# Where the scan's decay matrices come from: running sums spread by memory in place of segment sums by TensorE

## The chip, the cores and the metric

The kernel runs on one core of a Trainium2 chip. The metric is the device time of one execution, in microseconds (us). The kernel before took 1235.95 us (median of 3 runs, 1234.91 to 1236.33). Its engines are TensorE (PE, with its weight loads as PEld), VectorE (DVE), ScalarE (ACT), GpSimd (POOL) and SyncE (SP, which issues every DMA of this kernel).

## The reference

One layer of a hybrid encoder over 1024 prompt tokens and 64 sample tokens, width 1024. A projection gives z, x/B/C, dt and the input of a pooling branch; x/B/C go through a causal convolution and SiLU; then the chunked scan, a gate and an output projection; a SwiGLU feed-forward; and a gated per-layer embedding. The change is in the scan, whose core is:

```python
acum = cumsum(dtc * a, axis=time)             # running sum of the decay exponents of a chunk, per head
diff = acum[..., :, None] - acum[..., None, :]
lmat = exp(where(causal, diff, -inf))         # decay from token j to token i of the chunk
y_diag = einsum('bcign,bcjgn,bcgrij,bcjgrp->bcigrp', cc, bc, lmat, xdt)
decay_end = exp(acum[..., -1:] - acum)        # and chunk_decay = exp(acum[..., -1])
```

There are 8 heads. All of `dtc * a` is negative, so `acum` falls along a chunk.

## The kernel before

The kernel holds activations as [feature, token]. The 1088 tokens stand in four column groups of 272 for the large products. Each fp32 operand of those is split into a high and a low float32r part, and a product is three passes (high x high, high x low, low x high), run by `run` (L472, matmuls on L477). The scan takes 128 tokens at a time: 8 chunks of the prompt (c = 0 to 7) and one of the 64 sample tokens (c = 8).

The order of the instructions on PE, DVE, ACT and POOL is written out in advance by a planner, the class `Layout`. Jobs are Python generators that yield either a condition or a request: an engine, a cost in us, and a time to wait (`("A", 0.24, 0)`: ACT, 0.24 us, at once; "D" is DVE, "P" PE, "S" the issue of a DMA). The planner keeps a clock that moves on with each large product and with each "P" request, takes the ready jobs by priority, and emits an instruction when it gives a job its turn. So the costs decide the order, and the engines then run in this order, each waiting on semaphores for what it needs. DMAs stand on SP's single queue. What a DMA's reader is told to wait for is worked out by `dma` (L381) from a number of columns that the call names.

Scan chunks are jobs between the large products of the input projection. Before them, `dt_chain` (L957) computes for all 72 columns (9 chunks x 8 heads) the step `dt` and the exponent `dta`, and from three products with constant matrices (`le`: token j <= i, `gt`: token j > i, `ones`; L1018) by one exponential each `ea` (decay since the chunk's start), `dend` (to its end) and `cdec` (of the whole chunk).

`decay(c)` (L1036) prepares the decay matrices of a chunk on ACT: for each of 8 heads it multiplies the 128x128 matrix `le` by the head's column of `dta`, once for the high part (`dh`) and once for the low part (`dl`): 16 instructions. `ssd(c)` (L1049) then does, in this order: transposes and B/C products on PE (L1063 to L1068), `xdt`, `bk`, `cbm` (L1071 to L1079), **the segment sums on PE (L1089)**, four matmuls of 512 columns of the constant `gt_r` with `dh` and `dl`, into two PSUM banks; `xw` (L1092); the exponential of those banks into `e` on ACT (L1098); the skip term on ACT (L1103); the products with the state and for the new state (L1109, L1115); `e` times `cbm` (L1119), `yo`, the state's decay on DVE; and the chunk's output on PE (L1140, L1144). After its end the job of the next chunk is spawned; `decay(c + 1)` is spawned after `xw` of chunk c.

The chunks' results are gated by z (`z_job`, L1279; `gate`, L1296), and the output projection, the feed-forward (L1624, with a fast matrix scheme of seven products) and the embedding follow. Beside the scan runs the pooling branch (`pool_post`, L1190; its products on L1230).

Of the kernel before, what the change touches and what calls it, by code (L numbers as in the profile page):

```python
# [7 lines left out]
F32 = mybir.dt.float32  # L8
F32R = mybir.dt.float32r
I32 = mybir.dt.int32  # L10
AF = mybir.ActivationFunctionType
ALU = mybir.AluOpType
PSUM = bass.MemoryType.PSUM

P = 128
# [6 lines left out]
NC = len(CH)  # L22
# [300 lines left out]

@with_exitstack
def trunk(ctx, tc, xT, par, wmix, wdt, poolw, wout, wff, wdn, wpg, wpp, pT, ssm0,
          yT, ssm_o, conv_o, pool_o, h1_d, pool_d, e_d, af_d):
    nc = tc.nc
    ve, ac, gp, pe, sy = nc.vector, nc.scalar, nc.gpsimd, nc.tensor, nc.sync
    ET = mybir.EngineType
# [2 lines left out]
    const = ctx.enter_context(tc.tile_pool(name="const", bufs=1))  # L332
# [14 lines left out]
    banks = Banks()  # L347
    nts = Sem(NNT)
# [7 lines left out]
    def jbank(name):  # L356

        b = banks.take()
        return banks.hold(psall[:, b, :], b)
# [14 lines left out]
    def nt(name, dtype=F32):  # L374
        nts.take()
        return ntp.tile([P, CW], dtype, tag="nt", name=name)
# [4 lines left out]
    def dma(dst, src, cols):  # L381
        sy.dma_start(dst, src)
        return lay.load(cols)
# [4 lines left out]
    def pcol(name, i=None, n=1):  # L388
        a, b = _PCOLS[name]
        if i is None:  # L390
            return cp[:, a:b]
        return cp[:, a + i:a + i + n]

    gt_r = const.tile([P, P], F32R, name="gt_r")
    ident = pcol("ident")
    ones = pcol("ones")
    le = pcol("le")
    gt = pcol("gt")
# [439 lines left out]
            wsem.give()  # L838

    def gt_job():  # L840
        yield ("A", 0.2, 10)
        ac.copy(gt_r, pcol("gt"))
        yield ("D", 0.16)
        ve.tensor_tensor(pcol("pool_b"), pcol("pool_b"), pcol("pool_scale"), ALU.mult)

    spawn(w0_job(), 0)
# [88 lines left out]
    NH = 8 * NSSD  # L935

    def ct_(name):
        return keep.tile([P, NH], F32, name=name)

    dt, dta, dta_l, ea, dend, cdec = (ct_(n) for n in ("dt", "dta", "dta_l", "ea", "dend", "cdec"))  # L940
    dta_h = keep.tile([P, NH], F32R, name="dta_h")
    pwr = nt("pwr0"), nt("pwr1")
    dt_done = []

# [12 lines left out]
    def dt_chain():  # L957
        yield lambda: sdt[0] == 1 + NC
        yield banks.ok
        psd = jbank("psd")  # L960
        yield ("P", 1.0, 2)
        for c in range(NSSD):
            L = P if c < 8 else DEC
            pe.matmul(psd[:L, 8 * c:8 * c + 8], dtT[:, P * c:P * c + L], pcol("dtsum"),
                      start=True, stop=True)
        yield room_nt(3)
        s1, s2, s3 = (nt(f"sp{i}")[:, :NH] for i in range(3))
        d = ("D", 0.2, 0)
        yield ("D", 0.14, 1)
        ve.memset(dt, 0.0)  # L970
        by_c = "p (c h) -> p c h"
        ve.tensor_tensor(dt[:, :64].rearrange(by_c, h=8), psd[:, :64].rearrange(by_c, h=8),
                         pcol("dt_bias").unsqueeze(1).broadcast_to([P, 8, 8]), ALU.add)
        yield d
        ve.tensor_tensor(dt[:DEC, 64:72], psd[:DEC, 64:72], pcol("dt_bias")[:DEC], ALU.add)
        banks.give(psd)

        yield d
        ve.scalar_tensor_tensor(s1, dt, -1.0, dt, ALU.mult, ALU.max)
        yield ("A", 0.46)  # L980
        ac.activation(s1, s1, AF.Exp, scale=-1.0)
        ac.activation(ea[:, :8], pcol("a_log"), AF.Exp)
        yield ("D", 0.14, 2)
        ve.tensor_scalar(s2, s1, 2.0, None, ALU.add)
        yield ("D", 0.5)
        ve.reciprocal(s2, s2)
        yield d
        ve.tensor_tensor(s1, s1, s2, ALU.mult)
        yield d
        ve.tensor_tensor(s2, s1, s1, ALU.mult)  # L990
        yield d
        ve.tensor_scalar(s3, s2, 1.0 / 17, 1.0 / 15, ALU.mult, ALU.add)
        for k in (13, 11, 9, 7, 5, 3, 1):
            yield d
            ve.tensor_tensor(s3, s3, s2, ALU.mult)
            yield d
            ve.tensor_scalar(s3, s3, 1.0 / k, None, ALU.add)
        yield d
        ve.tensor_tensor(s3, s3, s1, ALU.mult)
        yield d  # L1000
        ve.tensor_scalar(dt, dt, 0.0, None, ALU.max)
        yield d
        ve.scalar_tensor_tensor(dt, s3, 2.0, dt, ALU.mult, ALU.add)
        ve.memset(dt[DEC:, 64:72], 0.0)
        yield d
        ve.scalar_tensor_tensor(dta.rearrange(by_c, h=8), dt.rearrange(by_c, h=8), -1.0,
                                ea[:, :8].unsqueeze(1).broadcast_to([P, NSSD, 8]), ALU.mult, ALU.mult)
        yield ("A", 0.2)
        ac.copy(dta_h, dta)
        yield ("D", 0.14)  # L1010
        ve.tensor_tensor(dta_l, dta, dta_h.bitcast(F32), ALU.subtract)
        for _ in range(3):
            nts.give()
        yield banks.ok
        psc = jbank("psc")
        yield ("P", 0.4, 2)
        for n, m in enumerate((le, gt, ones)):
            pe.matmul(psc[:, 128 * n:128 * n + NH], m, dta, start=True, stop=True)  # L1018
        yield ("A", 0.7)
        for n, o in enumerate((ea, dend, cdec)):  # L1020
            ac.activation(o, psc[:, 128 * n:128 * n + NH], AF.Exp)
        banks.give(psc)
        dt_done.append(1)

    spawn(dt_chain(), P_DTC)
# [8 lines left out]
    DD = {}  # L1034

    def decay(c):  # L1036

        L = DEC if c == 8 else P
        for g in range(2):
            hg = slice(8 * c + 4 * g, 8 * c + 4 * g + 4)  # L1040
            for nm, src in (("dh", dta_h.bitcast(F32)), ("dl", dta_l)):
                for h in range(4):
                    yield ("A", 0.24, 0)
                    if not h:
                        d = sp.tile([P, 4, P], F32R, tag=nm, bufs=2, name=f"{nm}{c}_{g}")
                    ac.activation(d[:L, h, :L], le[:L, :L], AF.Identity, scale=src[:L, hg][:, h:h + 1])
                DD[c, g, nm] = d

    def ssd(c):  # L1049
        sample, first = c == 8, c == 0  # L1050
# [28 lines left out]
        ve.tensor_tensor(cbm[:L, :, :L], pb[:L, 256:256 + 2 * L].rearrange("p (g i) -> p g i", g=2),  # L1079
                         le[:L, :L].unsqueeze(1).broadcast_to([L, 2, L]), ALU.mult)  # L1080
        banks.give(pb)
        yield lambda: banks.free >= 2 and (c, 1, "dl") in DD
        pgs = [jbank(f"pg{c}_{g}") for g in range(2)]
        es = []
        pvs = [p_[:L, :4 * L].rearrange("p (h i) -> p h i", h=4) for p_ in pgs]
        yield ("P", 0.9, 0)
        for g in range(2):
            for j, nm in enumerate(("dh", "dl")):
                pe.matmul(pvs[g], gt_r[:L, :L], DD[c, g, nm][:L, :, :L], start=j == 0, stop=j == 1)  # L1089
        yield ("D", 0.7, 0)  # L1090
        xw = sp.tile([P, 8, 64], F32, tag="xw", bufs=1, name="xw" + n)
        ve.tensor_tensor(xw[:L], xdt[:L], dend[:L, h8].unsqueeze(2).broadcast_to([L, 8, 64]), ALU.mult)  # L1092
        if c + 1 < NSSD:
            spawn(decay(c + 1), P_DEC)
        for g in range(2):
            yield ("A", 0.55, 1 - g)
            e = sp.tile([P, 4, P], F32, tag="e", name=f"e{c}_{g}")
            ac.activation(e[:L, :, :L], pvs[g], AF.Exp)  # L1098
            banks.give(pgs[g])
            es.append(e)  # L1100
        for b in range(4):
            yield ("A", 0.24, 0)
            ac.activation(xs[:, b, t0:t0 + L], xs[:, b, t0:t0 + L], AF.Identity, scale=pcol("d_skip", b))  # L1103
# [1244 lines left out]
```

## Time and profile before

| | |
|---|---|
| median of 3 runs | 1235.95 us |
| the profiled execution | 1235.68 us, its span 1233.8 us |
| PE busy, weight loads busy | 1208.4 us (98%), 1186.7 us (96%) |
| DVE, ACT, POOL busy | 873.2 us (71%), 596.1 us (48%), 69.4 us (6%) |
| segment sums (L1089) | 36 matmuls between 133 and 266 us |

The span runs from the first to the last instruction; the execution's time is 1.9 us more. An engine's share says how long it was busy, not whether others waited for it. PE is the one that is almost never idle; where a stage shows it busy all the time, only what PE itself does, or what it is made to wait for, can move the end. The views used below are the page's busy times, the busy times by stage, single instructions in order of time, the groups of instructions by line, the waits, and the DMA issues with their time to landing. For PE a matmul's length in the views includes a modelled end that overlaps the next matmul, so what a matmul costs in a stream is read from start to start.

### The profile page before, as it was taken

What the parts mean: (1) busy time and instruction counts of PE and PEld (TensorE: products, weight loads), DVE (VectorE), ACT (ScalarE), POOL (GpSimd) and SP (SyncE); (2) the same over time, 40 slices, a digit from 0 to 9 for tenths busy, and PEclk for the clock granted to TensorE, in tenths of its full rate; (3) what the DMA queues carried; (4) which work ended last, traced back from release to release, by engine and by line L of the source; (5) the groups of instructions that cost most, each with busy time, mean ns of one, the idle gap of its engine ahead of it and who ended that gap; (6) DMA issues with size and microseconds to landing.
All of it is one profiled execution on the core that took longest, in us unless ns stands there. A gap on an engine that the chain in (4) does not pass through costs nothing.

```text
span 1233.8 us, 23914 instructions
## 1 busy us (share of the span) xinstructions
PE 1208.4 (98%) x9676; PEld 1186.7 (96%) x9676; DVE 873.2 (71%) x1572; ACT 596.1 (48%) x1196; POOL 69.4 (6%) x56
## 2 busy tenths in 40 slices
PE   8999999999999999999999999999999999999997
PEld 6999999999999899999999999999999999999996
DVE  6696866785788786775767677666656555688875
ACT  6365667975546544444444444344433111356543
POOL 2000000111222100000000000000000000001111
PEclk8999999999999999999999999999999999999998
DMA  6121112124444233533443444336987666334422
GB/s 225 41 73 35 46 53 74 37 83 135 157 146 161 94 110 138 168 128 133 174 145 116 151 150 169 118 120 226 397 325 254 247 233 233 124 111 128 135 84 82
DMA packets 72399, 177.82 MB, mean 144 GB/s; under 512 B 8545, under 2 KB 16993, under 8 KB 72289
## 3 DMA queue, kind: packets, MB, share of 16 engines
q1 hardware_dynamic: 72288, 176.30, 41.5%
q8 instruction: 75, 1.23, 0.4%
q14 instruction: 36, 0.29, 0.1%
HBM read 117.31 MB, written 58.96 MB: 143 GB/s over the span
## 4 chain that ended last, share of the span: by engine, by line
PE 63%; DVE 3%; DMA 1%; ACT 0%; POOL 0%; issue 0%; DVEq 0%; ACTq 0%; POOLq 0%; SPq 0%
PE psall L1624 54%; PE psall L477 6%; PE psall L494 2%; POOL mixf L1414 0%; DVE f L1887 0%; PE psall L512 0%; DMA raw_pg<-in_wpg_dram 0%; DVE mixf L1439 0%; DVE sq_f L609 0%; PE psall L550 0%; DMA e_dram<-e 0%; DVE mixf L1408 0%; DVE mixf L1471 0%; DVE h_T L401 0%; PE psall L2107 0%
## 5 line engine op out<-in xcount | busy, mean ns | idle before, releaser
L477 PE MATMUL psall<-x,w_in 128*128 128x272 f32 x1440 | 194.9, 291 | 0.0
L477 PEld LDWEIGHTS psall<-x,w_in 128*128 128x128 f32 x1440 | 184.7, 188 | 4.0 <-issue 2.4
L1887 DVE TENSOR_TENSOR f<-f,psall 128x544 f32<-128x544 f32 (+1 forms) x96 | 60.7, 637 | 69.2 <-PE psall L1624 67.5
L1624 PE MATMUL psall<-h_T,w_g_S 128*128 128x272 f32 x792 | 103.0, 290 | 2.2 <-DVE h_T L401 1.8
L1624 PEld LDWEIGHTS psall<-h_T,w_g_S 128*128 128x128 f32 x792 | 101.3, 191 | 2.6 <-DVE h_T L401 2.0
L1624 PE MATMUL psall<-al_T,w_d_S 128*128 128x272 f32 x768 | 100.1, 288 | 0.9 <-DVE f L1887 0.5
L1624 PE MATMUL psall<-h_T,w_u_S 128*128 128x272 f32 x792 | 100.7, 287 | 0.0
L1624 PEld LDWEIGHTS psall<-h_T,w_u_S 128*128 128x128 f32 x792 | 99.6, 188 | 0.0
L1624 PEld LDWEIGHTS psall<-al_T,w_d_S 128*128 128x128 f32 x768 | 97.7, 188 | 1.6 <-DVE f L1887 0.7
L477 PE MATMUL psall<-mix,w_out 128*128 128x272 f32 x720 | 93.3, 289 | 0.0
L477 PEld LDWEIGHTS psall<-mix,w_out 128*128 128x128 f32 x720 | 90.9, 188 | 0.0
L1624 PE MATMUL psall<-al_B,w_d_A 128*128 128x272 f32 x528 | 72.1, 289 | 2.6 <-DVE w_d_A L401 2.6
L477 PE MATMUL psall<-h,w_pg 128*128 128x272 f32 x576 | 74.3, 289 | 0.0
L477 PEld LDWEIGHTS psall<-h,w_pg 128*128 128x128 f32 x576 | 72.7, 188 | 0.0
L1624 PEld LDWEIGHTS psall<-al_B,w_d_A 128*128 128x128 f32 x528 | 68.4, 188 | 3.1 <-DVE w_d_A L401 3.1
L1624 PE MATMUL psall<-h_B,w_g_A 128*128 128x272 f32 x528 | 70.2, 288 | 0.1
L1624 PE MATMUL psall<-h_B,w_u_A 128*128 128x272 f32 x528 | 69.7, 288 | 0.0
L1624 PEld LDWEIGHTS psall<-h_B,w_g_A 128*128 128x128 f32 x528 | 67.7, 188 | 0.4 <-ACT e L1807 0.4
L1624 PEld LDWEIGHTS psall<-h_B,w_u_A 128*128 128x128 f32 x528 | 67.5, 188 | 0.0
L1552 ACT CAST w_d_A<-raw_d 128x512 fp32r<-128x512 f32 (+3 forms) x44 | 22.3, 522 | 69.9 <-PE psall L1624 35.1
L1552 ACT CAST w_d_S<-raw_d 128x512 fp32r<-128x512 f32 (+3 forms) x54 | 26.5, 532 | 57.7 <-DVE raw_d L1576 33.6
L2073 POOL TENSOR_TENSOR f<-f,sq_f 128x544 f32<-128x544 f32 x5 | 7.4, 1482 | 726.8 <-DVE f L2070 721.4
(405 smaller groups left out, 2290.1 us busy)
## 6 DMA issues: line engine op xcount, KB each, us to landing
af_dram<-a_T SPq DMA_DIRECT2D x88, 272.0 KB, 2.3
al_T<-af_dram SPq DMA_DIRECT2D x44, 544.0 KB, 5.6
af_dram<-a_B SPq DMA_DIRECT2D x66, 272.0 KB, 2.3
al_B<-af_dram SPq DMA_DIRECT2D x33, 544.0 KB, 5.8
raw_g<-in_wff_dram SPq DMA_DIRECT2D x22, 512.0 KB, 4.2
raw_u<-in_wff_dram SPq DMA_DIRECT2D x22, 512.0 KB, 3.6
raw_in<-in_wmix_dram SPq DMA_DIRECT2D x15, 512.0 KB, 3.6
raw_d<-in_wdn_dram SPq DMA_DIRECT2D x14, 512.0 KB, 4.9
```

The costliest lines, as they stand in the source:

```text
L477: pe.matmul(out, lhsT, rhs, start=i == 0, stop=i == n - 1)
L494: pe.matmul(out, w.v(wi, k), act.v(xi, k, L), start=first and n == 0, stop=not left and n == 2)
L1552: ac.copy(v[:, 0], src)
L1624: pe.matmul(d[:, p - q.ps[0], :], w.v(wi, k), u.b(bf, xi, p, k), start=start and not k and not wi and not xi, stop=k == u.ks - 1 and wi == ...
L1887: ve.tensor_tensor(v[:, sl], v[:, sl], src[:, pl], ALU.add)
L2073: gp.tensor_tensor(v, v, hr, ALU.add)
```

## The change

The segment sum from token j to token i is the difference of two running sums, `acum[i] - acum[j]`. The changed kernel no longer forms it with `gt_r` on PE. `dt_chain` copies the `le` product to `acum` on ACT, transposes it on PE into the free end of the same bank (72 rows of heads, 128 tokens), copies that to SBUF on DVE, and stores it to a DRAM tensor `ac_d`. `decay(c)` loads the 8 rows of its chunk back, each lane getting the same 8 x 128 numbers, into `e` (three buffers); ACT then computes for each head `relu(acum[j] - acum[i])`, with `acum[j]` as the lane's bias (8 instructions of 128 columns), and `exp` of its negative (2 instructions of 512 columns). What `ssd` multiplies by `cbm` is this `e`; `cbm` is masked by `le`, so the entries that the relu cut to zero fall away. `gt_r`, `dta_h`, `dta_l`, the 16 products of ACT per chunk, the four matmuls and their two banks are gone. `dt_done`, which starts the scan, is now set after the store's landing as the planner reckons it.

```diff
-    gt_r = const.tile([P, P], F32R, name="gt_r")
...
-    dt, dta, dta_l, ea, dend, cdec = (ct_(n) for n in ("dt", "dta", "dta_l", "ea", "dend", "cdec"))
-    dta_h = keep.tile([P, NH], F32R, name="dta_h")
+    dt, dta, acum, ea, dend, cdec = (ct_(n) for n in ("dt", "dta", "acum", "ea", "dend", "cdec"))
...
-        s1, s2, s3 = (nt(f"sp{i}")[:, :NH] for i in range(3))
+        s1w, s2, s3 = (nt(f"sp{i}") for i in range(3))
+        s1, s2, s3, s1w = s1w[:, :NH], s2[:, :NH], s3[:, :NH], s1w[:, NH:NH + P]
...
-        yield ("A", 0.2)
-        ac.copy(dta_h, dta)
-        yield ("D", 0.14)
-        ve.tensor_tensor(dta_l, dta, dta_h.bitcast(F32), ALU.subtract)
-        for _ in range(3):
+        for _ in range(2):
             nts.give()
         yield banks.ok
         psc = jbank("psc")
         yield ("P", 0.4, 2)
         for n, m in enumerate((le, gt, ones)):
             pe.matmul(psc[:, 128 * n:128 * n + NH], m, dta, start=True, stop=True)
+        yield ("A", 0.2)
+        ac.copy(acum, psc[:, :NH])
+        yield ("P", 0.2, 0)
+        pe.transpose(psc[:NH, 384:512], acum, ident)
+        yield ("D", 0.2, 0)
+        ve.tensor_copy(s1w[:NH], psc[:NH, 384:512])
+        yield ("S", 0, 0)
+        at = dma(ac_d, s1w[:NH], 1)
         yield ("A", 0.7)
         for n, o in enumerate((ea, dend, cdec)):
             ac.activation(o, psc[:, 128 * n:128 * n + NH], AF.Exp)
         banks.give(psc)
+        yield ("A", 0.02, at)
+        nts.give()
         dt_done.append(1)
...
     def decay(c):
         L = DEC if c == 8 else P
+        yield ("S", 0, 0)
+        e = sp.tile([P, 8, P], F32, tag="e", bufs=3, name=f"e{c}")
+        at = dma(e, ac_d[8 * c:8 * c + 8].partition_broadcast(P), 2 * P)
+        for h in range(8):
+            yield ("A", 0.39, at if not h else 0)
+            ac.activation(e[:L, h, :L], e[:L, h, :L], AF.Relu, bias=acum[:L, 8 * c + h:8 * c + h + 1], scale=-1.0)
         for g in range(2):
-            hg = slice(8 * c + 4 * g, 8 * c + 4 * g + 4)
-            for nm, src in (("dh", dta_h.bitcast(F32)), ("dl", dta_l)):
-                for h in range(4):
-                    yield ("A", 0.24, 0)
-                    if not h:
-                        d = sp.tile([P, 4, P], F32R, tag=nm, bufs=2, name=f"{nm}{c}_{g}")
-                    ac.activation(d[:L, h, :L], le[:L, :L], AF.Identity, scale=src[:L, hg][:, h:h + 1])
-                DD[c, g, nm] = d
+            yield ("A", 0.55, 0)
+            ac.activation(e[:L, 4 * g:4 * g + 4, :L], e[:L, 4 * g:4 * g + 4, :L], AF.Exp, scale=-1.0)
+        DD[c] = e
...
-        yield lambda: banks.free >= 2 and (c, 1, "dl") in DD
-        pgs = [jbank(f"pg{c}_{g}") for g in range(2)]
-        es = []
-        pvs = [p_[:L, :4 * L].rearrange("p (h i) -> p h i", h=4) for p_ in pgs]
-        yield ("P", 0.9, 0)
-        for g in range(2):
-            for j, nm in enumerate(("dh", "dl")):
-                pe.matmul(pvs[g], gt_r[:L, :L], DD[c, g, nm][:L, :, :L], start=j == 0, stop=j == 1)
...
-        for g in range(2):
-            yield ("A", 0.55, 1 - g)
-            e = sp.tile([P, 4, P], F32, tag="e", name=f"e{c}_{g}")
-            ac.activation(e[:L, :, :L], pvs[g], AF.Exp)
-            banks.give(pgs[g])
-            es.append(e)
+        yield lambda: c in DD
+        es = DD[c][:, :4], DD[c][:, 4:]
```

The planner's order changes with it, from the end of `dt_chain` to the first groups of the output projection; after that the instructions of every engine stand as before. Three places show it. In the rows, names stand without buffer numbers, a trailing number is an instruction's own, and `x4` is a run of four.

On PE, in the kernel before, chunk 2 from the B/C products (L1067) to the products with the state (L1109) and for the new state (L1115):

```order
L1067 MATMUL psall<-ct,bt 128x128 x2
L477 MATMUL psall<-x_11_99,w_in_1458 128x272 x4
...
L477 MATMUL psall<-x_11_103,w_in_1458 128x272 x3
L1089 MATMUL psall<-dh_0_1828,gt_r 128x512
L1089 MATMUL psall<-dl_0_1834,gt_r 128x512
L1089 MATMUL psall<-dh_1_1848,gt_r 128x512
L1089 MATMUL psall<-dl_1_1873,gt_r 128x512
L477 MATMUL psall<-x_11_103,w_in_1458 128x272
...
L1109 MATMUL psall<-state_1846,ct 128x256 x2
L1115 MATMUL psall<-xw_1965,bk_1932 128x256 x2
```

On PE, in the changed kernel, chunk 3 over the same stretch (L1073 are the B/C products now, L1103 and L1109 those with and for the state):

```order
L1073 MATMUL psall<-ct,bt 128x128 x2
L476 MATMUL psall<-x_00_99,w_in_1452 128x272 x2
...
L476 MATMUL psall<-x_01_92,w_in_1591 128x272 x4
L476 MATMUL psall<-x_10_93,w_in_1591 128x272
L1103 MATMUL psall<-state_1894,ct 128x256 x2
L1109 MATMUL psall<-xw_1997,bk_1985 128x256 x2
```

The four long matmuls are gone, and fewer matmuls of the input projection stand between the two ends: 57 before, 39 now. Over the whole scan, the projection's work between one chunk's start and the next shrinks, and the ninth chunk's output stands 196 matmuls earlier in PE's order, 35 of them those that are gone less the one that is added.

On ACT, in the changed kernel, from chunk 1's `bk` (L1082) to chunk 2's; `e_1710` is chunk 2's decay, L1049 the relu and L1052 the exponential, L1097 the skip term, L1211 a step of the pooling branch:

```order
L1082 COPY bk_1684<-psall 128x256
L1097 ACTIVATE xs<-xs,cp 128x128 x4
L1049 ACTIVATE e_1710<-e_1710,acum 128x128 x3
L1211 CAST ph_1739<-s_3_1687 128x1103
L1049 ACTIVATE e_1710<-e_1710,acum 128x128 x5
L1052 ACTIVATE e_1710<-e_1710 128x512 x2
L447 CAST w_in_1795<-raw_in_1467 128x1024
L1230 ACTIVATE po_0_1800<-psall,cp 128x272
L1082 COPY bk_1829<-psall 128x256
```

Chunk 2's decay is whole before chunk 2's `bk`; before, its exponential stood behind `bk` and behind the segment sums. The table loads of ACT go from 19 to 15.

On SP, in the changed kernel, the store of the running sums and the broadcast loads (`e_1353`, `e_1576`, `e_1710`, `e_1853`, `e_2010` are chunks 0 to 4):

```order
L382 DMA raw_in_1199<-in_wmix_dram 128x1024
L382 DMA ac_dram<-sp_898 72x128
L382 DMA e_1353<-ac_dram 128x1024
L382 DMA e_1576<-ac_dram 128x1024
L382 DMA raw_in_1341<-in_wmix_dram 128x1024
L382 DMA e_1710<-ac_dram 128x1024
L382 DMA raw_in_1467<-in_wmix_dram 128x1024
L382 DMA out_conv_dram<-conv_out 128x48
L382 DMA raw_in_1605<-in_wmix_dram 128x1024
L382 DMA e_1853<-ac_dram 128x1024
L382 DMA e_2010<-ac_dram 128x1024
```

Ten DMAs are new: a store of 36 KB, on which the first load waits, and nine loads that write 512 KB each. The first three have a buffer at once; a later one waits until the chunk three before it has used its own. Weight loads (`raw_in`) stand between and behind them on the queue.

## Rows read from the trace of the kernel before

**Rows 1.** The page's busy time of each engine: us, share of the span, instructions.

```profile
...
PE 1208.4 (98%) x9676; PEld 1186.7 (96%) x9676; DVE 873.2 (71%) x1572; ACT 596.1 (48%) x1196; POOL 69.4 (6%) x56
```

**Rows 2.** Busy by stage: PE, PEld, DVE, ACT, POOL (instructions), clock, DMA share, GB/s.

```profile
...
150.00:170.00 20.00, 20.00 (x156) 19.14 (x155) 14.64 (x24) 13.68 (x40) 0.00 (x0) 1.00 0.16 55
...
190.00:210.00 20.00, 20.00 (x167) 18.85 (x166) 14.98 (x24) 14.38 (x32) 0.00 (x0) 1.00 0.19 61
210.00:230.00 20.00, 18.65 (x157) 17.73 (x156) 14.68 (x26) 17.33 (x46) 4.30 (x4) 1.00 0.20 60
230.00:250.00 20.00, 19.81 (x168) 18.87 (x167) 15.41 (x38) 18.54 (x50) 3.20 (x4) 1.00 0.13 36
...
290.00:310.00 20.00, 20.00 (x171) 20.00 (x171) 9.09 (x29) 7.60 (x18) 0.00 (x0) 1.00 0.30 94
```

**Rows 3.** PE in order of time, chunk 0: start us, us, instruction, count.

```profile
...
133.46 0.40 PE L1089 MATMUL psall<-dh,gt_r 128*128 128x512 f32 x1
133.69 0.39 PE L1089 MATMUL psall<-dl,gt_r 128*128 128x512 f32 x1
...
134.39 1.80 PE L477 MATMUL psall<-x,w_in 128*128 128x272 f32 x13
```

**Rows 4.** PE in order of time, chunk 8.

```profile
...
265.13 0.33 PE L1089 MATMUL psall<-dh,gt_r 64*64 64x256 f32 x1
...
265.74 1.01 PE L477 MATMUL psall<-x,w_in 128*128 128x272 f32 x6
```

**Rows 5.** Instructions of L1089: ns min/median/max, first and last start us, forms.

```profile
...
L1089 PE MATMUL psall<-dh,gt_r x18: 278/396/478, 133.5 to 265.4; 128*128 128x512 f32 x16, 64*64 64x256 f32 x2
```

**Rows 6.** PE in order of time, the products of the running sums.

```profile
...
106.92 0.79 PE L1018 MATMUL psall<-dta,cp 128*128 128x72 f32 x6
107.51 1.75 PE L477 MATMUL psall<-x,w_in 128*128 128x272 f32 x12
```

**Rows 7.** PE in order of time, four transposes of chunk 0.

```profile
...
130.10 0.60 PE L1063 MATMUL psall<-cp,xs 128*128 128x128 f32 x4
130.54 0.38 PE L1065 MATMUL psall<-cp,bt 128*128 128x128 f32 x2
```

**Rows 8.** ACT by group, 100 to 300 us: busy us, mean ns, idle before.

```profile
...
L1046 ACT ACTIVATE dh<-cp,dta_h 128x128 fp32r<-128x128 f32 x64 | 21.0, 395 | 0.0
...
L1098 ACT ACTIVATE e<-psall 128x512 f32<-128x512 f32 x16 | 8.7, 595 | 5.9 <-PE psall L1089 5.9
L1098 ACT ACT_TABLE_LOAD x6 | 7.7, 1283 | 0.1
```

**Rows 9.** ACT in order of time, chunk 6.

```profile
...
216.58 1.12 ACT L1217 CAST ph<-s 128x1103 fp32r<-128x1103 f32 x1 [2.26 <-DVE s L1212]
217.72 1.28 ACT L1098 ACT_TABLE_LOAD   x1
...
221.27 1.28 ACT L1288 ACT_TABLE_LOAD   x1
```

**Rows 10.** DVE in order of time, chunk 6.

```profile
...
223.03 0.44 DVE L1292 TENSOR_TENSOR xs<-xs,z 128x272 f32<-128x272 f32 x1 [3.64 <-ACT z L1288]
223.38 1.86 DVE L1119 TENSOR_TENSOR e<-e,cbm 128x512 f32<-128x512 f32 x2
```

**Rows 11.** PE in order of time, chunk 6's output.

```profile
...
226.00 0.63 PE L1140 MATMUL psall<-cp,yo 128*128 128x128 f32 x4 [1.35 <-DVE yo L1128]
```

**Rows 12.** DVE's waits, 150 to 170 us: us in total, times, longest.

```profile
...
DVE xs L1156 <- PE psall L1144: 3.3, 1, 3.3
```

**Rows 13.** ACT in order of time, end of the chain of dt.

```profile
...
107.79 1.28 ACT L1021 ACT_TABLE_LOAD   x1 [2.03 <-PE psall L1018]
```

**Rows 14.** DMA issues: count, KB each, median us from issue to landing.

```profile
...
al_B<-af_dram SPq DMA_DIRECT2D x33, 544.0 KB, 5.8
...
raw_in<-in_wmix_dram SPq DMA_DIRECT2D x15, 512.0 KB, 3.6
...
out_conv_dram<-conv_out SPq DMA_DIRECT2D x1, 24.0 KB, 1.5
```

More of the change, by code (lines that the diff above doesn't have):

```diff
@@ L325, in trunk @@
 def trunk(ctx, tc, xT, par, wmix, wdt, poolw, wout, wff, wdn, wpg, wpp, pT, ssm0,
-          yT, ssm_o, conv_o, pool_o, h1_d, pool_d, e_d, af_d):
+          yT, ssm_o, conv_o, pool_o, h1_d, pool_d, e_d, af_d, ac_d):
     nc = tc.nc
@@ L840, in gt_job @@
     def gt_job():
-        yield ("A", 0.2, 10)
-        ac.copy(gt_r, pcol("gt"))
-        yield ("D", 0.16)
+        yield ("D", 0.16, 10)
         ve.tensor_tensor(pcol("pool_b"), pcol("pool_b"), pcol("pool_scale"), ALU.mult)
@@ L2332 @@
     af_d = [nc.dram_tensor(f"af_{j}_dram", (7, P, 4 * CW), F32).ap() for j in range(NFF // 2)]
+    ac_d = nc.dram_tensor("ac_dram", (72, P), F32).ap()
     with tile.TileContext(nc) as tc:
@@ L2335 @@
               ap["wff"], ap["wdn"], ap["wpg"], ap["wpp"], [ap[f"p{c}"] for c in range(NC)], ap["ssm0"],
-              [ap[f"o_y{c}"] for c in range(NC)], ap["o_ssm"], ap["o_conv"], ap["o_pool"], h1_d, pool_d, e_d, af_d)
+              [ap[f"o_y{c}"] for c in range(NC)], ap["o_ssm"], ap["o_conv"], ap["o_pool"], h1_d, pool_d, e_d, af_d, ac_d)
     r = run_bass_kernel_spmd(nc, [feed], core_ids=[0])
```

## The prediction, made before the changed kernel was run

> **What bounds the kernel now.** The page's busy times come first: PE is busy 98% of the span, DVE 71%, ACT 48% [rows 1]. The busy time by stage, second, says where: PE works 20.00 of 20 us at full clock at 150 and 190 us, in the middle of the scan, while DVE has 14.64 and 14.98 and ACT 13.68 and 14.38 [rows 2]. From 210 to 250 us PE loses 1.35 and 0.19 us, where ACT is fullest (17.33 and 18.54); after the scan, at 290 us, PE is at 20.00 again with DVE at 9.09 and ACT at 7.60 [rows 2]. So in this stretch PE's own work sets the time, and others wait for it: between 150 and 170 us DVE stood 3.3 us for one output of the scan [rows 12]. Third, single instructions in order of time give what each removed or added one costs PE, from start to start. Fourth, the groups on ACT and the landing times of DMAs show whether what is added can hide.
>
> **PE, removed.** In chunk 0 the first segment sum starts at 133.46, the second at 133.69, and the projection goes on at 134.39: 0.23 us for one matmul of 512 columns, 0.93 us for four [rows 3]. Sixteen of the eighteen `dh` matmuls have 512 columns, and there are as many `dl` [rows 5]: eight chunks x 0.93 = 7.44 us. Chunk 8's four take 265.13 to 265.74, 0.61 us [rows 4]. Together 8.05 us.
>
> **PE, added.** One transpose of `acum`. Four transposes take 130.10 to 130.54, so 0.11 us each [rows 7]. It waits for ACT's copy. Before, ACT starts on the bank 0.87 us after PE's first of the three products (106.92 to 107.79) [rows 6, 13]; a copy of 72 columns is no row here, and lies between nothing and the 0.60 us of a 512-column exponential [rows 8]; I take 0.25. So `acum` is there 1.1 us after the products start. PE has 0.59 us of products, then six projection matmuls in the new order, each about 0.13 (12 in 1.75 us, less the last one's modelled end) [rows 6]: 1.4 us. The wait is nothing; ACT held by one convolution step would make it about 1.1 us, the length of a cast of similar width [rows 9]. Behind it on PE stands only the projection. Net for PE: 8.05 - 0.11 = 7.94 us.
>
> A rule of the Trainium skill speaks against the size of this term. "TensorE: Matmul & The Clock Gate", section "Back-to-back issue gap", gives about 131 ns per matmul of 512 columns in a stream of weight loads and matmuls, less than the 216 ns of one alone. By it, 32 x 0.131 + 0.61 = 4.8 us would go, and the gain would be 4.7 instead of 7.9, an estimate. The trace does not agree: each of its 512-column matmuls, with a weight load of its own, takes 0.23.
>
> **ACT.** Per chunk, 16 products of 128 columns become 8 relus of 128, and the two exponentials stay. The 64 full-size `dh` products keep ACT busy 21.0 us, 0.33 each [rows 8]. A relu with a per-lane bias does not occur; the nearest row is that product with a per-lane scale, and I take its 0.33 (0 to twice that: from 5 us less to no change in a chunk). So ACT does 8 x 0.33 = 2.6 us less a chunk, and four table loads of 1.28 us go [rows 8]. ACT's time lies beside PE's, and pays only where PE waited for it. Such a place is chunk 6: the pooling cast, then a table load at 217.72, the two exponentials, the skip term and the next table load at 221.27 [rows 9] kept DVE waiting 3.64 us for a z, so that `e` times `cbm` began at 223.38 [rows 10] and PE stood 1.35 us for `yo` [rows 11]. In the changed kernel the exponential is no longer between the segment sum and this product, but table loads still alternate with z's SiLU. I credit half, 0.7 us (0 to 1.54, all that PE loses from 210 to 250 us).
>
> **DMA and SP.** The store of 36 KB and chunk 0's load follow each other: nearest are 1.5 us (24 KB) and 3.6 us (512 KB of weights) [rows 14], so about 5 us. SP stands still for the first of these, with one weight load behind the first two broadcast loads. The running sums exist at about 108 us; chunk 0 wanted its segment sums at 133.46 [rows 3], so some 20 us of projection cover the round trip. Each later load is issued when the chunk three before has been used, with a chunk every 16.5 us (133.5 to 265.4 over eight) [rows 5]; after the change perhaps 13 us. It lands in 3.6 us, or 5.8 as in the busiest stretch [rows 14]: covered either way. That 128 lanes read the same 4 KB has no row; only a landing beyond some 13 us would be seen. Ten DMAs write 4.7 MB where the DMA engines are busy 0.13 to 0.20 [rows 2].
>
> **DVE.** One subtraction of 72 columns goes, one copy of 128 comes: nothing. But the chunks stand closer: per chunk 57 projection matmuls became 39 between the same two steps, 18 x 0.13 = 2.3 us, plus the 0.93. That is 3.3 of 16.5 us. DVE's share of 73 to 75% in the scan rises, to at most 93% if all its work moved together. I take 0.7 us of new waits on PE for this (0 to 4). After the scan, all engines' orders are as before and PE is full at 290 us, so what is gained is kept.
>
> **Sum.** The profiled execution took 1235.68 us: a span of 1233.8 and 1.9 around it. 1235.68 - 7.94 - 0.7 + 0.7 = 1227.7. The median of the runs is 0.27 above the profiled one: 1228.0 us.
>
> **Rivals.**
> 1. *Denser chunks make PE wait for DVE (slower).* Place: before each chunk's output (L1140), PE waits for `yo`, which is behind the two products with `cbm` (0.93 us each [rows 10]). With chunk starts 13 us apart each chunk would do what chunk 6 did, 1.35 us [rows 11]: nine times, 12.2 us, against 7.94: 1235.95 + 4.2 = 1240 us. It decides from 7.94 / 9 = 0.88 us per chunk on. For it: DVE is the second fullest engine. Against: the exponential that made chunk 6 late is out of this chain, and DVE waited for PE elsewhere. Chance 0.11.
> 2. *PE is paid by the matmul, not by the column.* Then 36 x 0.13 = 4.7 us go: 1231.3 us. For it: projection matmuls come every 0.13 us at 272 columns. Against: rows 3. The rule quoted above would give the same. Chance 0.05.
> 3. *The gain is given back.* PE reaches the output projection 8 us earlier and waits there for gates, whose chain of DVE and ACT has its own pace: about 1235.5 us. For it: ACT is nearly full from 230 to 250 us [rows 2]. Against: the scan ends still earlier against the projection than before, and ACT has less to do. Chance 0.08.
> 4. *The change's loads do not hide*, because the shared 4 KB comes slowly or the queue stands. At twice a chunk's 13 us, ACT would lose over 10 us on most of the chunks: above 1250 us. Against: rows 14. Chance 0.03.
>
> **How the numbers follow.** The forecast has 0.73, with its own range from 1225.5 (all of the 1.54 saved, no new waits, and 1 us for runs) to 1232 (4 us of new waits). Faster by over 0.2% (2.5 us, about what a measurement of this kernel can tell from no change) are the forecast and rival 2: 0.78; within it rival 3: 0.08; slower rivals 1 and 4: 0.14. The range to 1234 leaves out rivals 1 and 4 and most of 3.
>
> **What would show it.** Right: no 512-column matmul on PE between 130 and 270 us, PE at 20 of 20 through the scan, the first group of the feed-forward about 8 us earlier; relus of 0.3 to 0.4 us on ACT that wait for no DMA; broadcast loads landing in about 4 us. Wrong: waits of PE for `yo` or `e` beyond 0.9 us a chunk (rival 1); relus that wait for the load (rival 4); PE idle before the output projection (rival 3); a scan that ends 8 us earlier and an end that does not.

## The result, and the profile after

The changed kernel takes 1224.74 us in the median of 5 runs (1223.88 to 1226.61), beside 1235.95 for the kernel before. The ratio is 0.9916, 95% interval 0.9901 to 0.9932: 8.4 to 12.2 us less. Timed again later it gave 1226.25 us, ratio 0.9923 (0.9908 to 0.9937). So it is faster, as forecast; the forecast of 1228.0 was 3.3 us too slow, and the first median lies 0.8 us below the 1225.5 that the forecast gave as its own low end, while the second lies above it. Single runs of one kernel differ by some 2 us along with their mean granted clock: at 0.996 the kernel before took 1233.55 to 1234.08 us and the changed one 1223.88, at 0.993 they took 1235.50 to 1237.74 and 1226.21 to 1226.77.

The page of the changed kernel, busy time of each engine, to be held against [rows 1]:

```profile
...
PE 1200.6 (98%) x9641; PEld 1180.8 (96%) x9641; DVE 872.8 (71%) x1572; ACT 571.8 (47%) x1119; POOL 69.4 (6%) x56
```

PE has 7.8 us less, ACT 24.3 us less, DVE the same. The profiled run took 1226.61 us, the longest of its five, with a span of 1224.8: 9.0 us under the span before. Where these 9 us went shows best if the execution is cut at two marks that both kernels have: the first product of the `dt` chain (`psd`) and the first output projection. PE in the kernel before, the instructions of L964 and then the time order (columns as in [rows 5] and [rows 3]):

```profile
...
L964 PE MATMUL psall<-cp,ct x18: 170/256/256, 69.2 to 71.1; 128*128 128x8 f32 x16, 128*64 128x8 f32 x2
...
276.50 1.67 PE L1952 MATMUL psall<-mix,w_out 128*128 128x272 f32 x12
```

The same two marks in the changed kernel:

```profile
...
L960 PE MATMUL psall<-cp,ct x18: 170/256/256, 70.0 to 71.9; 128*128 128x8 f32 x16, 128*64 128x8 f32 x2
...
267.78 1.42 PE L1946 MATMUL psall<-mix,w_out 128*128 128x272 f32 x10
```

Between the marks: 276.50 - 69.2 = 207.3 us before, 267.78 - 70.0 = 197.8 after, 9.5 less. From the second mark to the end of the span: 957.3 before, 957.0 after. So in these two profiles the whole gain is made in the scan and none is given back. The first mark stands 0.8 us later in the changed run; over the runs below it stands between 68.9 and 71.2 us whatever was edited, so 1 to 2 us of difference ahead of it mean nothing.

The same stretches as in [rows 2], changed kernel:

```profile
...
150.00:170.00 20.00, 20.00 (x171) 19.12 (x170) 15.54 (x27) 11.17 (x31) 0.00 (x0) 1.00 0.33 108
190.00:210.00 20.00, 20.00 (x172) 19.12 (x171) 14.95 (x25) 14.00 (x28) 0.00 (x0) 1.00 0.33 113
210.00:230.00 20.00, 19.78 (x154) 18.80 (x153) 14.19 (x24) 17.75 (x46) 3.29 (x4) 1.00 0.19 57
230.00:250.00 20.00, 20.00 (x188) 18.04 (x187) 18.19 (x44) 12.53 (x34) 4.71 (x4) 1.00 0.29 87
290.00:310.00 20.00, 20.00 (x165) 20.00 (x164) 6.36 (x8) 9.12 (x16) 0.00 (x0) 1.00 0.34 107
```

PE stays at 20.00, and the two gaps from 210 to 250 us (1.35 and 0.19) are down to 0.22. That is all that PE waits between 70 and 270 us, by its waits (us in total, times, longest):

```profile
...
PE psall L1224 <- DVE pl L400: 0.2, 1, 0.2
```

So 7.9 (PE's work, net) + 1.54 (idle time gone) - 0.22 (new) = 9.3 of the 9.5 us. The step that the change removed is gone: PE in order of time, chunk 0 (compare [rows 3]):

```profile
...
132.29 2.79 PE L476 MATMUL psall<-x,w_in 128*128 128x272 f32 x21
134.91 1.02 PE L1109 MATMUL psall<-xw,bk 128*128 128x256 f32 x4
```

Projection runs up to the state product without a 512-column matmul between. And the new step on PE (compare [rows 6]):

```profile
...
107.01 0.78 PE L1011 MATMUL psall<-dta,cp 128*128 128x72 f32 x6
107.60 1.00 PE L476 MATMUL psall<-x,w_in 128*128 128x272 f32 x6
108.43 0.27 PE L1016 MATMUL psall<-cp,acum 128*72 128x128 f32 x1
```

No bracket behind L1016: the transpose waits for nothing, since six projection matmuls lie between. ACT in order of time at this place (compare [rows 13]):

```profile
...
107.83 0.22 ACT L1014 COPY acum<-psall 128x72 f32<-128x72 f32 x1 [3.52 <-PE psall L1011]
...
114.52 2.46 ACT L1049 ACTIVATE e<-e,acum 128x128 f32<-128x128 f32 x8 [2.48 <-DMA e<-ac_dram]
```

The copy took 0.22 us (taken: 0.25). The last row is the only relu that waits for a load, chunk 0's. SP's queue in order of time:

```profile
...
109.05 0.38 SPq L382 DMA_DIRECT2D ac_dram<-sp  x1
110.55 0.82 SPq L382 DMA_DIRECT2D e<-ac_dram  x2
```

From the store's issue to the first relu it is 5.5 us (taken: about 5), and chunk 0's product with `cbm` comes 21 us later, at 135.9. Landing times (compare [rows 14]):

```profile
...
e<-ac_dram SPq DMA_DIRECT2D x9, 512.0 KB, 3.9
```

ACT by group, 100 to 300 us (compare [rows 8]):

```profile
...
L1049 ACT ACTIVATE e<-e,acum 128x128 f32<-128x128 f32 x64 | 20.6, 392 | 2.5 <-DMA e<-ac_dram 2.5
...
L1052 ACT ACTIVATE e<-e 128x512 f32<-128x512 f32 x16 | 9.4, 622 | 0.0
...
L1052 ACT ACT_TABLE_LOAD x4 | 5.1, 1283 | 0.1
```

A full relu keeps ACT busy 20.6 / 64 = 0.32 us, as the product did (0.33). Note the last column of the exponentials: ACT no longer stands 5.9 us for a segment sum. Where chunk 6 was late is seen on three engines (compare [rows 9 to 11]). ACT in order of time, the exponentials of this chunk:

```profile
...
204.94 1.15 ACT L1052 ACTIVATE e<-e 128x512 f32<-128x512 f32 x2
```

DVE in order of time, their product with `cbm`:

```profile
...
212.62 1.28 DVE L1113 TENSOR_TENSOR e<-e,cbm 128x512 f32<-128x512 f32 x2
```

PE in order of time, the chunk's output:

```profile
...
217.57 0.60 PE L1134 MATMUL psall<-cp,yo 128*128 128x128 f32 x4
```

The exponentials end at 206.1, 6.5 us before DVE multiplies them with `cbm`, and 11 us before PE takes `yo`; neither row has a wait. In the kernel before, they and two table loads stood between z and its SiLU, for which DVE waited 3.64 us.

### The profile page after: what moved, and what is told of

Its sections match the earlier page's. It is cut to its first block, busy times and chain, and to the rows that moved or that the text cites. A ratio compares the mean times of both kernels' runs of the same rounds, so it can differ in the third digit from the quotient of the medians.

```text
span 1224.8 us, 23784 instructions
## 1 busy us (share of the span) xinstructions
PE 1200.6 (98%) x9641; PEld 1180.8 (96%) x9641; DVE 872.8 (71%) x1572; ACT 571.8 (47%) x1119; POOL 69.4 (6%) x56
## 4 chain that ended last, share of the span: by engine, by line
PE 62%; DVE 3%; DMA 2%; POOL 0%; ACT 0%; issue 0%; DVEq 0%; ACTq 0%; POOLq 0%; SPq 0%
PE psall L1618 54%; PE psall L476 6%; PE psall L493 2%; DMA al_B<-af_dram 1%; POOL mixf L1408 0%; DMA raw_d<-in_wdn_dram 0%; DVE f L1881 0%; PE psall L511 0%; DMA raw_pg<-in_wpg_dram 0%; DVE mixf L1433 0%; DVE sq_f L608 0%; PE psall L549 0%; DMA e_dram<-e 0%; DVE mixf L1402 0%; DVE mixf L1465 0%
## 5 line engine op out<-in xcount | busy, mean ns | idle before, releaser
L1618 PE MATMUL psall<-h_B,w_u_A 128*128 128x272 f32 x528 | 69.7, 288 | 0.0
```

What stands on the lines that cost most here:

```text
L1618: pe.matmul(d[:, p - q.ps[0], :], w.v(wi, k), u.b(bf, xi, p, k), start=start and not k and not wi and not xi, stop=k == u.ks - 1 and wi == ...
```

## The experiments

Two theories on the 9 to 11 us. **Columns:** PE is full in the scan, and the gain is the 7.9 us of matmuls; what happens on ACT and DVE matters little. **ACT:** a lighter ACT, with exponentials ready early, is a condition of the gain, since ACT was almost as full as PE at 210 to 250 us. Smaller rivals: PE is paid by the matmul; the loads only just hide. All edits but one (the kernel without segment sums) start from the changed kernel.

**1. Four 512-column matmuls put back per chunk** (their result is overwritten).

```
         yield ("P", 1.2, 0)
+        for _ in range(4):
+            pe.matmul(px[:L, :4 * L], pw[:L, 1, 0, :L], pw[:L, 0, :4, :L], start=True, stop=True)
```

> The changed kernel (1224.7 us) with four extra matmuls of 512 columns (chunk 8: 256) put in front of each chunk's transposes on PE; their results are overwritten at once, the order of everything else and the planner's costs stay. Theory (PE is the bound, and its matmuls cost what they take from start to start): the 8.05 us of the removed segment sums come back, 1232.8 us, between 1232 and 1234. Rival, PE is paid by the matmul and not by the column: 36 x 0.13 = 4.7 us, 1229.4. Rival, the gain comes from the shorter chain of a chunk and PE has room: 1225 to 1226.

Measured: 1233.70 us (11 runs), ratio to before 0.9981 (0.9972 to 0.9990). PE in order of time:

```profile
...
129.35 1.09 PE L1069 MATMUL psall<-pw 128*128 128x512 f32 x4
130.29 0.60 PE L1071 MATMUL psall<-cp,xs 128*128 128x128 f32 x4
```

From start to start 0.94 us for four, as the segment sums had (0.93), so 7.5 us for eight chunks; 7.5 to 9.0 us came back by the medians (1226.25 and 1224.74 without). Between the marks the profile has 205.4 us (69.7 to 275.1), 7.6 more than without, and PE waits for nothing there. Most of the gain is these columns, and rival 2 and the rival of an off-path PE fall.

**2. The same with 128 columns.**

```
         yield ("P", 1.2, 0)
+        for _ in range(4):
+            pe.matmul(px[:L, :1 * L], pw[:L, 1, 0, :L], pw[:L, 0, :1, :L], start=True, stop=True)
```

> As the run before, but the four extra matmuls per chunk have 128 columns (chunk 8: 64). Theory (columns count): at most the 0.11 us of a 128-column transpose each, at least a quarter of 0.23: 36 x 0.06 to 0.11 = 2.1 to 4.0 us, 1226.8 to 1228.7. Rival, paid by the matmul: 4.7 us, 1229.4, the same as with 512 columns.

Measured: 1228.91 us, ratio 0.9946 (0.9934 to 0.9959): 2.7 to 4.2 us above the changed kernel, which by itself can't separate the two prices. The trace can:

```profile
...
128.61 0.56 PE L1069 MATMUL psall<-pw 128*128 128x128 f32 x4
129.00 0.62 PE L1071 MATMUL psall<-cp,xs 128*128 128x128 f32 x4
```

0.39 us for four, 0.10 each, beside 0.23 for 512 columns: PE is paid neither by the column alone (a quarter of 0.235, 0.06) nor by the matmul alone (0.235 again). 36 x 0.10 = 3.5 us agrees with the time, and with the 3.4 us that the marks lie further apart (69.0 to 270.2, 201.2 us).

**3. ACT as full as before.** One more multiplication, by ones, ahead of each relu on the same piece, unknown to the order of work.

```
             yield ("A", 0.39, at if not h else 0)
+            ac.activation(e[:L, h, :L], e[:L, h, :L], AF.Identity, scale=ones[:L, 0:1])
```

> The changed kernel with ACT's load put back: each relu has one more instruction of 128 columns with a per-lane scale of one on the same tile in front of it, so 16 per chunk as before, and the order stays. Theory (what the vanished waits of PE needed was that the exponential left the chunk's chain): PE waits no more than now, 1224.7 to 1225.5 us. Rival (ACT's lighter load is what removed the waits of 1.5 us): they come back, 1226.2 us or more.

Measured: 1231.99 us (11 runs), ratio 0.9978 (0.9969 to 0.9986): 5.7 to 7.3 us lost, with the PE work unchanged. My theory, columns alone, fell here. PE's waits, 70 to 280 us:

```profile
...
PE psall L1225 <- ACT ph L1212: 2.5, 1, 2.5
PE psall L1074 <- ACT ct L895: 1.4, 1, 1.4
PE psall L1225 <- DVE pl L400: 1.0, 1, 1.0
PE psall L1110 <- DVE xw L1091: 0.3, 1, 0.3
```

5.2 us of waits, 3.5 of them for the pooling cast, which stands on ACT behind the relus with their partners, a table load and an exponential, and for the part that DVE makes from it. Between the marks the profile has 204.9 us (69.7 to 274.6), 7.1 more than without the edit. And the busy time of this kernel around the longest of them:

```profile
...
210.00:230.00 20.00, 16.18 (x125) 14.90 (x124) 10.63 (x17) 19.64 (x45) 2.23 (x3) 0.97 0.23 72
225.00:230.00 5.00, 1.50 (x8) 1.08 (x7) 1.31 (x1) 4.96 (x6) 0.14 (x1) 0.89 0.00 0
230.00:235.00 5.00, 5.00 (x33) 4.97 (x33) 3.60 (x7) 4.37 (x13) 1.07 (x1) 0.77 0.08 28
```

ACT is at 19.64 of 20. After PE stood 3.5 us of 5, its granted clock is 0.77 in the next 5 us although it is busy all of it. The edit also holds more than its load: the second of a pair on one piece waits for the first (2 x 0.32 = 0.64 us was meant, 0.73 measured), and nothing was told to the order. So two gentler versions followed.

**4. The same load, independent of the relu beside it, still unknown to the order.**

```
+            k = (h + 4) % 8
+            ac.activation(e[:L, k, :L], e[:L, k, :L], AF.Identity, scale=ones[:L, 0:1])
```

> The changed kernel with 8 more instructions of 128 columns per chunk on ACT, as in the earlier run with 16, but each on a head other than that of the relu in front of it, so that no pair depends on each other (there a pair took 0.73 us, here two should take 0.6); the order stays. Theory A: 1224.7 to 1225.5. Theory B: PE waits again between 210 and 250 us, less than in the earlier run: 1227 to 1231 us.

Measured: 1227.65 us, ratio 0.9941 (0.9929 to 0.9953). PE waited 0.9 us for `pl` and 0.8 for `ph`, 1.7 against 0.2, and ACT had 18.84 of 20 in 210 to 230 us. The marks lie 199.9 us apart (68.9 to 268.8), 2.1 more than without; the two profiles of the changed kernel and that of experiment 9 have 197.7 to 197.8.

**5. The same load as steps of their own, which the order plans.**

```
+            ac.activation(e[:L, h, :L], e[:L, h, :L], AF.Identity, scale=ones[:L, 0:1])
+        for h in range(8):
+            yield ("A", 0.39, 0)
```

> The same ACT load, but the 8 instructions stand in front of the 8 relus and each is a request of its own to the planner (0.39 us), so the order is planned with it. Theory A: 1224.7 to 1226. Theory B: the planner spaces the chunks as ACT allows and fills PE with projection, so less than the untold load costs, 1225.5 to 1229, with the chunks later than in the changed kernel.

Measured: 1228.39 us, ratio 0.9940 (0.9927 to 0.9953). Here the marks are not further apart (69.4 to 267.4, 198.0 us), but eight transposes of a gate (`t_g`, some 0.5 us) stand behind the second mark and not ahead of it, and the rest of the span is 2.7 us longer (959.7 against 957.0). The longer wait lies there, at these transposes. PE in order of time:

```profile
...
247.23 0.69 PE L549 MATMUL psall<-cp,t_g 68*128 68x68 f32 x8 [0.23 <-DVE t_g L545]
274.74 0.69 PE L549 MATMUL psall<-cp,t_g 68*128 68x68 f32 x8 [1.14 <-DVE t_g L545]
```

Numbers 4 and 5 agree on the size, 1.4 to 3.7 us by the medians for 8 products a chunk. Their intervals overlap those of both timings of the changed kernel (up to 0.9932 and 0.9937), so the times alone don't show a loss; the new waits are there in the traces, one profile each.

**6. The exponentials back in the chunk's chain,** ACT's work as in the changed kernel.

```
         yield lambda: c in DD
+        e = DD[c]
+        for g in range(2):
+            yield ("A", 0.55, 0)
+            ac.activation(e[:L, 4 * g:4 * g + 4, :L], e[:L, 4 * g:4 * g + 4, :L], AF.Exp, scale=-1.0)
```

> The changed kernel with the two exponentials of a chunk put back to where they were, in the chunk's own chain behind xw, and only load and relus done ahead. ACT's work is the same as in the changed kernel. Theory: the exponential in the chain, with its table load, makes PE wait again once or more in the part of the scan where z's SiLU alternates with it: 1225.5 to 1227 us, and PE's wait for yo is back. Rival (ACT's load): no difference, 1224.7.

Measured: 1228.76 us, ratio 0.9945 (0.9931 to 0.9959), slower than either theory had it. The wait for `yo` came back as 0.27 us only, and a larger one stands elsewhere:

```profile
...
226.61 0.69 PE L549 MATMUL psall<-cp,t_g 68*128 68x68 f32 x8 [1.69 <-DVE t_g L545]
...
245.36 0.66 PE L1135 MATMUL psall<-cp,yo 128*128 128x128 f32 x4 [0.27 <-DVE yo L1123]
```

DVE in the same kernel shows what `t_g` was late for:

```profile
...
225.06 0.44 DVE L1287 TENSOR_TENSOR xs<-xs,z 128x272 f32<-128x272 f32 x1 [2.50 <-ACT z L1283]
225.41 0.15 DVE L535 TENSOR_TENSOR t_g<-t_g 68x8 f32<-68x8 f32 x1
```

On ACT the table load, two exponentials, the skip term and another table load ran from 219.67 to 224.59 before z's SiLU could start. It is the pattern of chunk 6 in the kernel before [rows 9, 10], with another PE instruction at its end. The granted clock was 0.81 and 0.85 in the two stretches of 5 us from 225 on, and the marks lie 200.9 us apart (71.2 to 272.1), 3.1 more than without the edit.

**7. The kernel before without its 36 segment-sum matmuls;** the exponentials read the products directly, so that the decays are not the reference's.

```
-        for g in range(2):
-            for j, nm in enumerate(("dh", "dl")):
-                pe.matmul(pvs[g], gt_r[:L, :L], DD[c, g, nm][:L, :, :L], start=j == 0, stop=j == 1)
...
-            ac.activation(e[:L, :, :L], pvs[g], AF.Exp)
+            ac.activation(e[:L, :, :L], DD[c, g, "dh"][:L, :, :L].bitcast(F32), AF.Exp)
```

> The kernel before without the segment sums: the 36 matmuls and their banks are left out, and the exponential reads the high product (dh) from SBUF instead, so that the decays are not the reference's; the 16 products per chunk on ACT, the exponential in the chunk's chain and all else stay, planned anew. Theory A (PE's columns are the gain, ACT has room): 1235.8 - 8.05 = 1227.7 us or a little less, 1227 to 1228.5. Theory B (with PE's columns gone ACT's 16 products and the late exponential hold the chunks between 200 and 250 us, and what PE waits there also lowers its clock): 1229 to 1232 us, with PE waits of 1 us and more and a granted clock below 1.00 in that stretch.

Measured: 1229.54 us (7 runs, 1228.39 to 1233.97), ratio 0.9959 (0.9944 to 0.9973). PE's side of the change alone, with ACT left heavy, brings 3.3 to 6.9 us where 8.05 were taken off PE. All of PE's waits from 220 to 300 us:

```profile
...
228.52 0.69 PE L550 MATMUL psall<-cp,t_g 68*128 68x68 f32 x8 [1.23 <-DVE t_g L546]
246.41 0.66 PE L1133 MATMUL psall<-cp,yo 128*128 128x128 f32 x4 [1.37 <-DVE yo L1121]
277.08 0.71 PE L550 MATMUL psall<-cp,t_g 68*128 68x68 f32 x8 [1.62 <-DVE t_g L546]
```

In its profile the first output projection comes 7.8 us sooner after the first mark than before, and the rest of the span is 4.3 us longer (961.6 against 957.3). Of these, 1.62 are the last wait; about 1.7 are the clock, an estimate from 0.92 and 0.91 in the two 10 us behind the mark (1.00 in the kernel before); and some 0.5 are eight transposes of a gate that stand ahead of the mark in the kernel before. The profiled run took 1232.72 us, 3.2 more than the median, so in most runs less is lost. This is a part of what rival 3 says, at a gate's transpose, with ACT at 19.93 of 20 us (210 to 230) and 19.51 (230 to 250).

**8. One buffer for the loads in place of three.**

```
-        e = sp.tile([P, 8, P], F32, tag="e", bufs=3, name=f"e{c}")
+        e = sp.tile([P, 8, P], F32, tag="e", bufs=1, name=f"e{c}")
```

> The changed kernel with one buffer for the decays instead of three: a chunk's broadcast load can go out only when the chunk before has used its own, while the planner still believes it lands 2.5 us after it is asked for. Theory (the loads cost nothing because they are issued more than a chunk ahead): now 3.9 us of landing, 2.5 us of relus and 1.1 us of exponentials stand between one chunk's end and the next chunk's product with cbm, against some 8 us from a chunk's end to that product in the order, and ACT, which waits for the load in order, holds up what stands behind it: slower by 3 to 40 us, with ACT waiting for the loads in most chunks. Rival (the load's lead doesn't matter): 1224.7.

Measured: 1279.00 us, ratio 1.0356 (1.0341 to 1.0372); 53 to 54 us lost, more than the 40 I allowed at most. ACT now waits 7 to 12 us for each of the eight later loads; two of the rows, in order of time:

```profile
...
199.27 2.45 ACT L1049 ACTIVATE e<-e,acum 128x128 f32<-128x128 f32 x8 [7.04 <-DMA e<-ac_dram]
...
215.32 0.98 ACT L1049 ACTIVATE e<-e,acum 128x128 f32<-128x128 f32 x3 [9.72 <-DMA e<-ac_dram]
```

The two largest of PE's waits behind them, 70 to 280 us, and two stretches of its busy time:

```profile
...
PE psall L1224 <- ACT ph L1211: 13.0, 2, 7.6
PE psall L1224 <- DVE pl L400: 7.7, 4, 6.0
...
130.00:170.00 40.00, 30.00 (x203) 27.71 (x202) 21.50 (x35) 16.12 (x40) 0.00 (x0) 0.84 0.12 41
...
250.00:290.00 40.00, 25.59 (x186) 23.33 (x186) 16.83 (x38) 21.73 (x53) 3.25 (x4) 0.79 0.22 70
```

The relu stands on ACT's queue for its load, and casts that PE needs stand behind it. This is rival 4 as it would have looked.

**9. Two buffers, and the changed kernel once more,** on one chip.

```
-        e = sp.tile([P, 8, P], F32, tag="e", bufs=3, name=f"e{c}")
+        e = sp.tile([P, 8, P], F32, tag="e", bufs=2, name=f"e{c}")
```

> The changed kernel with two decay buffers in place of more, so that a chunk's broadcast loads still start a chunk ahead. Theory (a chunk of lead, some 20 us, covers loads of 3.9 us): the same as the changed kernel, 1224 to 1227 us, no PE wait on the decays. Rival (any shortening of the lead costs, as the single buffer did with 54 us): 1230 to 1260 us, with PE waiting for ACT at the state products and the granted clock under 0.95 in the scan.

> The changed kernel once more, nothing edited, as the measure for the other runs and for how far a second sitting moves it. Theory (the gain is 7.9 us of PE columns and some 1.5 us of PE waits in the scan): 1224 to 1227 us, 9 to 11 us under the kernel before, with 197 to 199 us from the scan's first product to the first output projection. Rival (the first runs were a lucky sitting, the gain is the columns alone): 1227.5 to 1229 us.

Measured: 1225.47 us with two buffers (ratio 0.9919, 0.9903 to 0.9936) and 1226.25 unedited. Both have the same single wait of 0.2 us on PE in the scan; the unedited one has its marks at 70.0 and 267.79, the same 197.8 us between. One chunk of lead covers the loads in full; the third buffer buys nothing. The two-buffer profile has 197.7 between its marks (69.6 and 267.34) and a span of 1222.9, 2.0 less than the unedited one: 0.4 ahead of the first mark and 1.5 behind the second, where the kernels do the same. The 1.5 us behind the mark come from one place in the feed-forward. PE in order of time and its busy time there, first the unedited kernel and then two buffers:

```profile
...
418.46 6.18 PE L1618 MATMUL psall<-h_T,w_g_S 128*128 128x272 f32 x35 [1.82 <-DVE h_T L400]
...
413.00:423.00 10.00, 7.79 (x48) 7.36 (x47) 8.37 (x10) 4.47 (x7) 0.00 (x0) 0.83 0.00 0
...
418.02 4.68 PE L1618 MATMUL psall<-h_T,w_g_S 128*128 128x272 f32 x35 [1.83 <-DVE h_T L400]
...
413.00:423.00 10.00, 7.79 (x60) 7.36 (x59) 9.55 (x11) 5.51 (x8) 0.00 (x0) 1.00 0.00 0
```

The same wait and the same 35 matmuls took 1.50 us more in one run, at a granted clock of 0.83 in place of 1.00. The first profile of the changed kernel and those of experiments 4 to 7 have the longer time here (6.04 to 6.19 us), those of experiments 1 to 3 the shorter (4.68); why the clock fell in one run and not in another, no run shows. So the scan's gain is steady, and totals move by 2 us with what lies outside it.

## Why the prediction was right, and which terms were off

- **PE, removed (8.05) and added (0.11).** Right. The matmuls are gone; put back they cost 0.94 per four and 7.5 to 9.0 us in all. The transpose waits for nothing.
- **The price of a 512-column matmul.** The step measured 0.23 us before and 0.235 in experiment 1. By the 131 ns of the Trainium skill ("TensorE: Matmul & The Clock Gate", section "Back-to-back issue gap") the 32 full matmuls of experiment 1 would have cost 4.2 us, an estimate. The trace does not agree with that figure for these matmuls: eight times 0.94 us are 7.5.
- **ACT, "I credit half, 0.7 us".** Mis-sized: all of the 1.54 us went. The exponentials of chunk 6 are over 6.5 us before their use, so it was not a question of half.
- **DMA and SP, "covered either way".** Right: landing took 3.5 to 7.2 us, 3.9 in the median (taken: 3.6 or 5.8), only chunk 0's relus waited, and PE and DVE did not wait for what came of them. The lead is what does it (experiment 8).
- **DVE, "0.7 us of new waits on PE for this (0 to 4)".** Mis-sized: 0.22. The denser chunks are real: the state products of chunks 0 and 7 stand 93.9 us apart (134.91 and 228.81), 13.4 a chunk (taken: 13; before, 137.79 to 254.89, 16.7). The 57 and 39 projection matmuls behind that estimate are of chunk 2 before and chunk 3 after; over chunks 1 to 8 the traces count 49 and 33 in the mean, so the step to 13 came out right although its count did not set like against like. DVE's busy time from 130 to 210 us rose from 57.16 to 63.01 of 80 us. But it still waits for PE, 1.7 us once and 1.5 in two between 150 and 170 us (compare [rows 12]):

```profile
...
DVE yo L1122 <- PE psall L1103: 1.7, 1, 1.7
DVE xs L1150 <- PE psall L1138: 1.5, 2, 0.8
```

- **The two together.** I set +0.7 against -0.7, so that the sum was PE's work alone. They measure -1.54 and +0.22. That makes 7.94 + 1.32 = 9.3 us, or 1226.4 by the profiled run, which took 1226.61. The first median's other 1.7 us have no place in the profiled run. The second timing of the same kernel lacks them, experiment 9 shows where single runs gain or lose 1.5 us by the clock, and the four other first runs have a mean clock of 0.994 to 0.996 beside the profiled one's 0.993. That theirs is the same scatter fits these figures, but without their profiles it is not shown.
- **"ACT's time ... pays only where PE waited for it."** True for the change, but incomplete. It reads ACT's relief only from waits that the profile of before shows. With PE faster and ACT left or made about as full as before, PE met waits of 1.7 to 5.2 us (experiments 3, 4 and 7), and in 3 and 7 a lower clock behind them. ACT's relief paid for these too, without a row in the trace of before.
- **Rivals.** Rival 1's danger is real, but on the wrong engine: the queue that runs full when chunks move together is ACT's (19.93 of 20 in experiment 7), and DVE is late behind it. A part of what rival 3 says happens with ACT not relieved (experiments 5 and 7). Rival 4 appears as soon as the loads have no lead. In the changed kernel none shows. It does three things at once: fewer columns on PE, fewer products on ACT, and a chain that runs ahead of the chunk. The experiments took these away one at a time, and each cost time or brought waits.

Open: how the ACT term divides between fewer products and early exponentials. Each alone was taken away, at 1.4 to 4.0 us by the medians, with intervals too wide to add or order them.

## What to carry to other kernels

When the bounding engine is relieved, ask of the next fullest engine, in the very stretch, whether it could carry the same work in the shorter time: here ACT, at 17 to 18.5 of 20 us, went to 19.5 to 19.9 when PE alone was relieved, and PE's saving came to 3.3 to 6.9 us in place of 8.4 to 12.2. Take a step out of the chain of a chunk by computing it from data that exist early, and give it one chunk of lead: one buffer cost 53 us, two were as good as three. Waits in the profile of before price what disappears; what the faster engine would meet next has to be worked out from the fullness of its neighbours.

## What the runs showed of the hardware

- A wait of PE can cost more than itself. In experiment 3, PE's granted clock was 0.89 in the 5 us in which it stood 3.5, and 0.77 in the next 5, in which it was busy throughout; in experiment 8 two stretches of 40 us ran at 0.79 and 0.84. 0.77 is a mean between the two levels, 2.4 and 1.2 GHz. In the scan of the kernel before and of the changed one the granted clock was 1.00, in the former with its wait of 1.35 us [rows 2, 11].
- The same wait did not always lower the clock. After 1.82 and 1.83 us at the same place, 35 matmuls took 6.18 us in one run and 4.68 in another, at 0.83 and 1.00 (experiment 9).
- A load that spreads 4 KB of memory over 128 lanes (512 KB written) landed in 3.9 us in the median, about as loads of 512 KB of distinct weights did (3.6).
- A matmul with a weight load of its own, from start to start in a full stretch at a granted clock of 1.00: 0.10 us at 128 columns, 0.125 at 272 (21 in the 2.62 us from 132.29 to 134.91), 0.235 at 512.
- An exponential of 512 columns took 0.62 us in place, and 0.60 when it read the matmul's bank [rows 8].
